# Sixteen per-head stores of the sliding attention's bias table during the difference attention, in place of one store during the projections

## The chip, the cores and the metric

The kernel runs on one core of one Trainium2 chip. Its engines are TensorE (PE, with weight loads as a queue of their own, PEld), VectorE (DVE), ScalarE (ACT), GpSimd (POOL) and SyncE (SP), which here only issues DMA transfers; 16 DMA engines carry them out. The metric is device time in microseconds (us); smaller is better.

## The reference, cut to what matters

Two transformer blocks in fp32 over 2048 tokens of width 1024. The first projects the normed input into eight chunks of 512 columns, runs a difference attention (4 heads) and a dilated attention (8 heads), gates both and adds a projection. The second is a causal sliding-window attention with 16 heads, window 128, a learned bias by distance and a sink for each head. That bias is what the change is about:

```python
def first_block(x, ...):
    u = rms_norm(x, mix_norm_g) @ w_in
    dq, dk, dv, bq, bk, bv, z = jnp.split(u, IN_SPLIT_IDX, axis=-1)
    ...
    a = diff_attention(dq, dk, dv, lam, diff_slopes)     # softmax 0 minus lam * softmax 1, times v
    b = dilated_attention(bq, bk, bv, dil_slopes)
    y = jnp.concatenate([a, b], axis=-1) * jax.nn.silu(z)
    ...
def banded_attention(q, k, v, t5_table, window, sinks):
    ...
    dist = nprev * Q_BLOCK + jnp.arange(Q_BLOCK)[:, None] - jnp.arange(kc)[None, :]
    valid = (dist >= 0) & (dist < window) & (kpos >= 0)
    bias = jnp.take(t5_table, t5_bucket(dist), axis=0)
    s = jnp.where(valid, s + bias, NEG)
    ...
```

The bias depends on the distance alone, so a head's whole bias matrix is made from one vector of 384 numbers: 128 of bias in the middle and −1e30 on both sides.

## The kernel before, in words

The program is a row of phases: `phase_a` (projections), `phase_b1` (difference attention), `phase_b2` (dilated attention), `phase_c` (output projection and gate), `phase_d` (sliding attention) and `phase_e`. Intermediate results go through DRAM tiles named `s_...`. A scheduler with a timeline of its own puts each engine's instructions into a fixed order; semaphores do the rest. All transfers named here are issued by SP, in SP's order, on one queue (`q1` in the profile).

**Projections.** `phase_a` takes the eight chunks in the order dv, bv, dk, dq, bk, bq, z0, z1, and in each chunk 16 tiles of 128 tokens. A tile is 24 matmuls (8 blocks of depth, three products of high and low parts, L190 to L192) into one of four PSUM buffers `psm`. In the second half of a chunk the next chunk's weights are loaded: SP fetches `wraw` (3 buffers, L98), ACT makes the high part (L100) and POOL the low part (L101). In the chunks dv and bv a tile leaves PSUM like this, one store for each part:

```python
            raw = wrp.tile([P, 512], F32, name="wraw")                                       # L97
            nc.sync.dma_start(raw, w_in[0, k * P:(k + 1) * P, ch * 512:(ch + 1) * 512])      # L98
            w = wp.tile([P, 2, 512], F32R, name="w")
            nc.scalar.activation(w[:, 0], raw, AF.Copy)                                      # L100
            ...
            nc.scalar.activation(ev[0], psv, AF.Copy, scale=rs)                              # L110
            nc.vector.scalar_tensor_tensor(ev[1], psv, rs, ev[0].bitcast(F32), ...)          # L111
            for i in range(2):
                nc.sync.dma_start(scr[nm][rows][:, :, i], ev[i].bitcast(F32))                # L113
```

**The bias table.** After the first chunk `phase_a` calls `prep_swa`. It fills `e_vec`, 16 partitions (one for each head) of 384 numbers, and stores it to `s_toep`, 16 x 128 x 384 numbers in DRAM: each head's row is written 128 times, 3 MB in one transfer (L978). `phase_d` reads it skewed by one number from row to row, which turns the repeated vector into the bias matrix.

**Difference attention.** `phase_b1` works through 64 tiles `g` of 128 queries, 16 for each of 4 heads. PE computes scores (L331) from `kst` and `qst`, DVE adds distances and takes the maximum, ACT takes the exponentials, and POOL combines the two softmaxes in halves (L364, L365). Three tiles later PE transposes the result (L375), and pairs of tiles are multiplied by `vt` (L389 to L391). Every fourth tile `finish` loads a gate block `b_sz` (L404), multiplies it on POOL (L406), multiplies the output by it (L418) and stores the output to `s_y` (L419). The next head's `kst` (L305) and `vt` (L311) are loaded at the boundary between heads, `qst` (L318) every fourth tile.

Of the kernel before, what the change touches and what calls it, by code (L numbers as in the profile page):

```python
# [7 lines left out]
F32 = mybir.dt.float32  # L8
# [8 lines left out]
P = 128  # L17
# [251 lines left out]
def phase_b1(tc, c, scr, ndist, sub_g, lam):  # L269
    nc = tc.nc  # L270
    NQ = 4 * NT
    with (
# [27 lines left out]
        def load_k(h, e, j):  # L300
            for i in range(2):
                t = (kp0 if heads["n"] % 22 < 20 else kp1).tile([P, 512], F32R, name="kst")
                heads["n"] += 1
                for half in range(2):
                    nc.sync.dma_start(t[64 * half:64 * half + 64].bitcast(F32),  # L305
                                      scr["dk"][h, e, i][:, j * 512:j * 512 + 512])
                heads[h, "k", e, i, j] = t

        def load_v(h, j):
            t = vp.tile([P, 4, 2, 128], F32R, name="vt")  # L310
            nc.sync.dma_start(t.bitcast(F32),  # L311
                              scr["dv"][j * 512:(j + 1) * 512, h].rearrange("(k p) i w -> p k i w", p=P))
            heads[h, "v", j] = t

        def load_q(h, b):
            for e in range(2):
                t = (qp0, qp1)[b % 2].tile([P, 512], F32R, name="qst")
                nc.sync.dma_start(t.bitcast(F32),  # L318
                                  scr["dq"][h, e].rearrange("s d t -> (s d) t")[:, b * 512:b * 512 + 512])
                qts[h, b, e] = t  # L320

        def scores(g, e, hf):
            h, qt = divmod(g, NT)
            if e == 0 and hf == 0:
                st[g] = {"e": [pool.tile([P, 2, 1024], F32, name="et") for pool in (tp1 if g % 4 == 3 else tp0, tp3 if g % 3 == 2 else tp2)], "l": sp.tile([P, 2], F32, name="l")}
            et = st[g]["e"][e]
            lhs = qts[h, qt // 4, e][:, (qt % 4) * P:(qt % 4 + 1) * P]
            ps = ps_s.tile([P, 1024], F32, name="s_ps")
            for b in range(2):
                for i in range(2):  # L330
                    nc.tensor.matmul(ps[:, b * 512:b * 512 + 512], lhs, heads[h, "k", e, i, 2 * hf + b],  # L331
                                     start=i == 0, stop=i == 1)
            if hf == 0:
                st[g]["mx"] = sp.tile([P, 2], F32, name="mx")
            mx = st[g]["mx"]
            off = 1920 - qt * P + hf * 1024
            nc.vector.tensor_tensor_reduce(  # L337
                et[:, hf], ps, bias[:, off:off + 1024], 1.0,
                -3.0e38 if hf == 0 else mx[:, 0:1], ALU.add, ALU.max, mx[:, hf:hf + 1])

        def exps(g, e):
            slope = DIFF_SLOPES[g // NT]
            et, mx = st[g]["e"][e], st[g]["mx"]
            nm = sp.tile([P, 1], F32, name="nm")
            nc.scalar.activation(nm, mx[:, 1:2], AF.Copy, scale=-slope)
            ev = et.rearrange("p a k -> p (a k)")
            nc.scalar.activation(ev, ev, AF.Exp, bias=nm, scale=slope, accum_out=st[g]["l"][:, e:e + 1])  # L347
# [45 lines left out]
        def evacuate(p):  # L393
            ot = op.tile([P, 256], F32, name="b_ot")
            nc.scalar.activation(ot, outs.pop(p), AF.Copy)
            outs[p, "t"] = ot
# [29 lines left out]
        for g in range(NQ + LT + 5):  # L426
            h, qt = divmod(g, NT)
            if g < NQ and qt == 0:
                for j in range(4):
                    load_v(h, j)  # L430
            if g < NQ and qt % 4 == 1:
                ng = g + 3
                if ng < NQ:
                    load_q(ng // NT, (ng % NT) // 4)
            for s in range(4):
                e, hf = divmod(s, 2)
                if g < NQ:
                    with tc.high_priority(offset=AHEAD) if g < EARLY else nullcontext():
                        scores(g, e, hf)
                    if qt == NT - 1 and h < 3 and hf == 1:  # L440
                        for j in range(4):
                            load_k(h + 1, e, j)
                if 0 <= g - LT < NQ:
                    transposes(g - LT, s)
                p, half = divmod(g - LT - 2, 2)
                if 0 <= p < NQ // 2:
                    for kt in range(8 * half + 2 * s, 8 * half + 2 * s + 2):
                        pv(p, kt)
                if s == FIN and half == 0 and 0 <= p - 1 < NQ // 2:
                    finish(p - 1)  # L450
                if g < NQ and hf == 1:
                    with tc.high_priority(offset=AHEAD) if g < EARLY else nullcontext():
                        exps(g, e)
            if g < NQ:
                with tc.high_priority(offset=AHEAD) if g < EARLY else nullcontext():
                    combine(g)
            p, half = divmod(g - LT - 2, 2)
            if half == 1 and 0 <= p < NQ // 2:
                evacuate(p)
        ssq = c["ssq"].rearrange("p h t -> p (h t)")  # L460
        rsqrt_dve(nc, fp, ssq, 128, ssq)

# [497 lines left out]
def prep_swa(tc, c, scr, table, onehot, sinks, pm):  # L960


    nc = tc.nc
    sk8 = c["const"].tile([P, 16], F32, name="e_sk")
    nc.sync.dma_start(sk8, sinks.broadcast_to([P, 16]))
    nc.vector.tensor_scalar(sk8, sk8, 8.0, None, ALU.mult)
    c["sk8"] = sk8
    with tc.tile_pool(name="p_c", bufs=1) as cp:
        tb = cp.tile([32, 16], F32, name="e_tb")
        nc.sync.dma_start(tb, table)  # L970
        oh = cp.tile([32, P], F32, name="e_oh")
        nc.sync.dma_start(oh, onehot)
        vec = cp.tile([16, 384], F32, name="e_vec")
        nc.vector.memset(vec, -1.0e30)
        ps = pm.tile([P, 512], F32, name="pst")[:16, :P]
        nc.tensor.matmul(ps, tb, oh, start=True, stop=True)
        nc.vector.tensor_scalar(vec[:, 128:256], ps, 8.0, None, ALU.mult)
        nc.sync.dma_start(scr["toep"], vec.unsqueeze(1).broadcast_to([16, P, 384]))  # L978


def phase_d(tc, c, scr, a_w_in):
# [310 lines left out]
def diff_lambda(tc, c, lams):  # L1292
    nc = tc.nc
    c["lam"] = c["const"].tile([P, 1], F32, name="lam")
    with tc.tile_pool(name="l_c", bufs=1) as cp:
        lt = cp.tile([P, 4, 64], F32, name="lt")
        for i, ap in enumerate(lams):
            nc.sync.dma_start(lt[:, i], ap.broadcast_to([P, 64]))
        pr = cp.tile([P, 2, 64], F32, name="lpr")
        for i in range(2):  # L1300
            nc.vector.tensor_mul(pr[:, i], lt[:, 2 * i], lt[:, 2 * i + 1])
        s2 = cp.tile([P, 2], F32, name="ls2")
        nc.vector.reduce_sum(s2, pr, axis=AX.X)
        nc.scalar.activation(s2, s2, AF.Exp)
        nc.vector.tensor_sub(c["lam"], s2[:, 0:1], s2[:, 1:2])
        nc.vector.tensor_scalar(c["lam"], c["lam"], LAM_INIT, None, ALU.add)
# [21 lines left out]
def kernel_body(tc, a, out):  # L1328
    with (
        tc.tile_pool(name="const", bufs=1) as cp,  # L1330
        tc.tile_pool(name="dram", bufs=1, space=DRAM) as dp,
    ):
        c = consts(tc, cp)
        scr = make_scratch(dp)
        phase_a(tc, c, a["x"], a["w_in"], a["mix_norm_g"],
                [a["diff_q_norm_g"], a["diff_k_norm_g"], a["dil_q_norm_g"], a["dil_k_norm_g"]], scr,
                lambda pm: [
                    diff_lambda(tc, c, [a["lambda_q1"], a["lambda_k1"], a["lambda_q2"], a["lambda_k2"]]),
                    prep_swa(tc, c, scr, a["t5_table_2"], a["t_onehot"], a["a_sinks_2"], pm)])
        phase_b1(tc, c, scr, a["t_ndist"], a["diff_sub_norm_g"], c["lam"])  # L1340
        phase_b2(tc, c, scr, a["t_nat"], a["t_res"], a["t_two"])
        phase_c(tc, c, scr, a["x"], a["p"], a["w_out"], a["ple_norm_g"], a["w_ple_gate"], a["w_ple_proj"],
                a["norm_g_2"])
        phase_d(tc, c, scr, a["a_w_in_2"])
        phase_e(tc, c, scr, a["a_w_out_2"], a["final_g_2"], out)
# [29 lines left out]
```

## Time and profile before

| what | value |
|---|---|
| median of 3 runs | 2956.58 us (2953.58 to 2958.02) |
| the profiled execution's own time | 2958.66 us |
| its span | 2956.9 us |
| PE busy | 2878.8 us (97%) |
| DVE, ACT, POOL busy | 1803.7 us (61%), 1562.5 us (53%), 1239.1 us (42%) |
| moved by DMA | 346.00 MB, 117 GB/s in the mean |

The profile is of one execution, which lies 2.1 us above the median. Busy shares are means over all phases. The timelines list one engine's instructions in order of time, with the idle time before an instruction and what ended it in square brackets; the windows give the busy time of each engine in a stretch, and the clock that PE was granted (1.00 is 2.4 GHz, 0.50 is 1.2 GHz).

### The profile page before, as it was taken

The numbers are of one execution on the slowest core, as the hardware profiler recorded it, in microseconds if no ns is written. First come the engines' busy times: TensorE is split into PE (matmuls) and PEld (weight loads), VectorE is DVE, ScalarE is ACT, GpSimd is POOL, SyncE is SP. The second block draws the span as 40 slices with busy tenths as digits, with TensorE's granted clock in tenths as the row PEclk, the third lists the DMA queues.
The fourth block names the chain that finished last, engine by engine and source line by source line (L and its number), as shares of the span: only waits on it lengthen the run. The fifth ranks groups of instructions, "written<-read, shape, count | busy, mean of one in ns | idle before, by whom it ended". The sixth has DMA issues, their size and how long they took to land.

```text
span 2956.9 us, 45164 instructions
## 1 busy us (share of the span) xinstructions
PE 2878.8 (97%) x15554; PEld 2455.2 (83%) x15554; DVE 1803.7 (61%) x4607; ACT 1562.5 (53%) x3480; POOL 1239.1 (42%) x1156
## 2 busy tenths in 40 slices
PE   9999999999999999989999899999999999999998
PEld 7878888888798888878999778888788888888787
DVE  4215556522688888887877654444535756666855
ACT  5222333221588888878989442222345756665621
POOL 1110111001488888864777700000156555555421
PEclk9999999999999999999999899999999999999999
DMA  6663444424314132129786633232554243332552
GB/s 208 116 160 86 122 114 121 96 87 115 121 30 115 46 106 65 51 64 189 143 164 133 180 116 110 77 113 92 183 166 155 86 157 96 109 100 72 156 182 79
DMA packets 410646, 346.00 MB, mean 117 GB/s; under 512 B 89745, under 2 KB 356401, under 8 KB 408497
## 3 DMA queue, kind: packets, MB, share of 16 engines
q1 hardware_dynamic: 388000, 329.24, 40.2%
q10 hardware_dynamic: 20736, 8.65, 1.8%
q0 software_dynamic: 1680, 5.21, 0.7%
q8 instruction: 124, 2.03, 0.3%
q14 instruction: 106, 0.86, 0.1%
HBM read 227.51 MB, written 116.52 MB: 116 GB/s over the span
## 4 chain that ended last, share of the span: by engine, by line
PE 86%; DMA 5%; DVE 3%; ACT 2%; SPq 1%; issue 1%; POOL 0%; DVEq 0%; ACTq 0%; POOLq 0%
PE s_ps L331 8%; PE psm L190 7%; PE psm L192 7%; PE psm L191 7%; PE e_mm L804 5%; PE e_mm L806 5%; PE e_mm L805 5%; PE c_mm L804 4%; PE c_mm L805 4%; PE c_mm L806 4%; PE t_ps L375 3%; PE o_ps L389 2%; PE o_ps L391 2%; PE o_ps L390 2%; PE d_sr L590 2%; PE f_mm L805 2%
## 5 line engine op out<-in xcount | busy, mean ns | idle before, releaser
L190 PE MATMUL psm<-w,hh 128*128 128x512 f32 x1024 | 406.3, 398 | 9.4 <-DVE t L111 8.0
L191 PE MATMUL psm<-w,hl 128*128 128x512 f32 x1024 | 399.5, 391 | 0.0
L192 PE MATMUL psm<-w,hh 128*128 128x512 f32 x1024 | 399.5, 393 | 0.0
L101 POOL TENSOR_TENSOR w<-wraw,w 128x512 fp32r<-128x512 f32 x64 | 81.5, 1294 | 600.2 <-ACT w L100 589.9
L365 POOL TENSOR_TENSOR et<-et 128x1024 f32<-128x1024 f32 x124 | 296.0, 2409 | 0.0
L331 PE MATMUL s_ps<-kst,qst 128*128 128x512 f32 x1024 | 289.7, 407 | 5.5 <-DVE mx L337 3.7
L347 ACT ACTIVATE et<-et,nm 128x2048 f32<-128x2048 f32 x128 | 257.2, 2009 | 5.2
L1026 POOL TENSOR_TENSOR e_wt<-e_raw,e_wt 128x1024 fp32r<-128x1024 f32 x80 | 191.3, 2399 | 111.9 <-ACT e_wt L1025 110.9
L190 PEld LDWEIGHTS psm<-w,hh 128*128 128x128 f32 x1024 | 193.5, 189 | 48.3 <-DVE t L111 8.4
L804 PE MATMUL e_mm<-e_x,e_wt 128*128 128x512 f32 x576 | 228.2, 396 | 1.2 <-DVE e_k L1068 0.8
L806 PE MATMUL e_mm<-e_x,e_wt 128*128 128x512 f32 x576 | 226.8, 394 | 0.0
L192 PEld LDWEIGHTS psm<-w,hh 128*128 128x128 f32 x1024 | 192.9, 189 | 40.9
L805 PE MATMUL e_mm<-e_x,e_wt 128*128 128x512 f32 x576 | 226.6, 393 | 0.0
L191 PEld LDWEIGHTS psm<-w,hl 128*128 128x128 f32 x1024 | 193.7, 189 | 38.2
L331 PEld LDWEIGHTS s_ps<-kst,qst 128*128 128x128 f32 x1024 | 175.9, 190 | 45.3 <-DVE mx L337 18.1
L1127 POOL TENSOR_SCALAR e_es<-e_es,e_l 128x256 f32<-128x256 f32 (+1 forms) x256 | 119.4, 485 | 170.8 <-DVE e_l L1125 118.6
L364 POOL TENSOR_SCALAR et<-et,cc 128x1024 f32<-128x1024 f32 x124 | 138.2, 1129 | 110.3 <-PE psm L192 57.1
L377 DVE TENSOR_TENSOR ptl<-t_ps,pth 128x512 fp32r<-128x512 f32 x256 | 169.4, 684 | 19.9 <-ACT pth L376 16.8
L337 DVE CUSTOM_DVE_ANT_0 et<-s_ps,nd,mx 128x1024 f32<-128x1024 f32 x128 | 163.9, 1280 | 26.5 <-PE s_ps L331 24.7
L1114 DVE CUSTOM_DVE_ANT_0 e_es<-e_s,e_bias,e_sk 128x256 f32<-128x256 f32 (+1 forms) x256 | 117.4, 473 | 102.6 <-PE e_s L1106 71.2
L376 ACT ACTIVATE pth<-t_ps 128x512 fp32r<-128x512 f32 x256 | 143.6, 595 | 44.8 <-PE t_ps L375 41.1
L850 POOL TENSOR_TENSOR c_yn<-c_yn,ssq_sub 128x512 f32<-128x512 f32 x16 | 17.0, 1061 | 354.1 <-DMA c_yn<-s_y 354.1
(268 smaller groups left out, 7848.2 us busy)
## 6 DMA issues: line engine op xcount, KB each, us to landing
e_raw<-in_a_w_in_dram SPq DMA_DIRECT2D x80, 512.0 KB, 3.7
wraw<-in_w_in_dram SPq DMA_DIRECT2D x64, 256.0 KB, 3.5
kst<-s_dk SPq DMA_DIRECT2D x128, 128.0 KB, 4.2
s_xt<-c_at SPq DMA_DIRECT2D x32, 512.0 KB, 6.8
e_x<-s_xt SPq DMA_DIRECT2D x32, 512.0 KB, 7.1
t<-in_x_dram SPq DMA_DIRECT2D x32, 256.0 KB, 5.4
s_dv<-t SPq DMA_DIRECT2D x32, 256.0 KB, 3.3
s_bv<-t SPq DMA_DIRECT2D x32, 256.0 KB, 3.6
```

What stands on the lines that cost most here:

```text
L190: nc.tensor.matmul(ps, ah, cur[k][:, 0], start=k == 0, stop=False)
L191: nc.tensor.matmul(ps, al, cur[k][:, 0], start=False, stop=False)
L192: nc.tensor.matmul(ps, ah, cur[k][:, 1], start=False, stop=k == KD - 1)
L331: nc.tensor.matmul(ps[:, b * 512:b * 512 + 512], lhs, heads[h, "k", e, i, 2 * hf + b], start=i == 0, stop=i == 1)
L337: nc.vector.tensor_tensor_reduce(et[:, hf], ps, bias[:, off:off + 1024], 1.0, -3.0e38 if hf == 0 else mx[:, 0:1], ALU.add, ALU.max, mx[:, ...
L347: nc.scalar.activation(ev, ev, AF.Exp, bias=nm, scale=slope, accum_out=st[g]["l"][:, e:e + 1])
L365: nc.gpsimd.tensor_sub(es[0][:, hf], es[0][:, hf], es[1][:, hf])
L377: nc.vector.tensor_sub(tl[:, :, qi], pt, th[:, :, qi].bitcast(F32))
L804: nc.tensor.matmul(ps, ah, bh, start=first, stop=False)
L805: nc.tensor.matmul(ps, al, bh, start=False, stop=False)
L806: nc.tensor.matmul(ps, ah, bl, start=False, stop=last)
L1026: nc.gpsimd.tensor_sub(w[:, 1], raw, w[:, 0].bitcast(F32))
```

## The change

`e_vec` moves to a pool of its own, `early`, that lives through the projections and the difference attention. The store of `prep_swa` is taken out, and 16 stores take its place in the loop of `phase_b1`: at the end of every even tile from 8 to 38, one head's row, written 128 times (192 KB) from one partition. `keep_in_program_order` keeps each where it is written relative to SP's neighbours.

```diff
@@ phase_b1, end of the loop over g
             p, half = divmod(g - LT - 2, 2)
             if half == 1 and 0 <= p < NQ // 2:
                 evacuate(p)
+            if g % 2 == 0 and 8 <= g < 40:
+                hd = (g - 8) // 2
+                tc.keep_in_program_order(nc.sync.dma_start(
+                    scr["toep"][hd], c["vec"][hd:hd + 1].unsqueeze(1).broadcast_to([1, P, 384])))
@@ prep_swa
-        vec = cp.tile([16, 384], F32, name="e_vec")
+        vec = c["early"].tile([16, 384], F32, name="e_vec")
         nc.vector.memset(vec, -1.0e30)
...
         nc.vector.tensor_scalar(vec[:, 128:256], ps, 8.0, None, ALU.mult)
-        nc.sync.dma_start(scr["toep"], vec.unsqueeze(1).broadcast_to([16, P, 384]))
+    c["vec"] = vec
@@ kernel_body
-        phase_a(tc, c, ...)
-        phase_b1(tc, c, scr, a["t_ndist"], a["diff_sub_norm_g"], c["lam"])
+        with tc.tile_pool(name="early", bufs=1) as c["early"]:
+            phase_a(tc, c, ...)
+            phase_b1(tc, c, scr, a["t_ndist"], a["diff_sub_norm_g"], c["lam"])
```

SP's order between the first and the second chunk of the projections, before (`s_dv` are stores of the first chunk, `s_bv` of the second, `wraw` the weights to come):

```order
L113 DMA s_dv<-t_1169 512x1x128
L98 DMA wraw<-in_w_in_dram 128x512 x3
L978 DMA s_toep<-e_vec 2048x1x384
L113 DMA s_dv<-t_1204 512x1x128
L98 DMA wraw<-in_w_in_dram 128x512
L113 DMA s_dv<-t_1205 512x1x128
L98 DMA wraw<-in_w_in_dram 128x512 x2
L113 DMA s_bv<-t_1270 1024x1x64
```

and after:

```order
L113 DMA s_dv<-t_1172 512x1x128
L98 DMA wraw<-in_w_in_dram 128x512 x3
L113 DMA s_dv<-t_1207 512x1x128
L98 DMA wraw<-in_w_in_dram 128x512
L113 DMA s_dv<-t_1208 512x1x128
L98 DMA wraw<-in_w_in_dram 128x512 x4
L113 DMA s_bv<-t_1272 1024x1x64
```

The store has left the queue, and two weight loads more stand ahead of the first store of the second chunk.

SP's order in the difference attention, from the first two `b_sz` loads to the `kst` loads of the second head, before:

```order
L404 DMA b_sz<-s_sz 128x4x128 x2
L318 DMA qst<-s_dq 128x512 x4
L419 DMA s_y_138<-b_an 128x4x128
L404 DMA b_sz<-s_sz 128x4x128
L318 DMA qst<-s_dq 128x512 x2
L419 DMA s_y_138<-b_an 128x4x128
L404 DMA b_sz<-s_sz 128x4x128
L305 DMA kst<-s_dk 64x512 x20
```

and after:

```order
L404 DMA b_sz<-s_sz 128x4x128
L462 DMA s_toep<-e_vec 128x1x384
L404 DMA b_sz<-s_sz 128x4x128
L462 DMA s_toep<-e_vec 128x1x384
L318 DMA qst<-s_dq 128x512 x4
L419 DMA s_y_138<-b_an 128x4x128
L462 DMA s_toep<-e_vec 128x1x384
L404 DMA b_sz<-s_sz 128x4x128
L318 DMA qst<-s_dq 128x512 x2
L419 DMA s_y_138<-b_an 128x4x128
L462 DMA s_toep<-e_vec 128x1x384
L404 DMA b_sz<-s_sz 128x4x128
L462 DMA s_toep<-e_vec 128x1x384
L305 DMA kst<-s_dk 64x512 x20
```

A store of one head now stands ahead of each of these `b_sz` loads but the first; the six loads that follow here have one ahead of them too, and the boundary to the third head has its two stores in the same places.

POOL's order around the sixth `b_sz` load, before:

```order
L418 TENSOR_TENSOR b_an<-b_an,b_sz 128x512
L364 TENSOR_SCALAR et<-et,cc 128x1024 x2
L406 TENSOR_TENSOR b_sz<-b_sz,g_6576 128x512
L365 TENSOR_TENSOR et<-et 128x1024 x2
L364 TENSOR_SCALAR et<-et,cc 128x1024 x2
```

and after:

```order
L418 TENSOR_TENSOR b_an<-b_an,b_sz 128x512
L364 TENSOR_SCALAR et<-et,cc 128x1024 x2
L365 TENSOR_TENSOR et<-et 128x1024
L406 TENSOR_TENSOR b_sz<-b_sz,g_6578 128x512
L365 TENSOR_TENSOR et<-et 128x1024
L364 TENSOR_SCALAR et<-et,cc 128x1024 x2
```

The multiply by the gate block has moved behind the first half of L365; the same holds for the seventh and the eighth load, and the other places keep their order. PE's order is the same in both kernels.

## Rows read from the trace of the kernel before

**Rows 1.** The page: busy time by engine, and shares of the chain.
```profile
PE 2878.8 (97%) x15554; PEld 2455.2 (83%) x15554; DVE 1803.7 (61%) x4607; ACT 1562.5 (53%) x3480; POOL 1239.1 (42%) x1156
...
PE 86%; DMA 5%; DVE 3%; ACT 2%; SPq 1%; issue 1%; POOL 0%; DVEq 0%; ACTq 0%; POOLq 0%
```

**Rows 2.** DMA issues, 110 to 160: operation, count, size, us from issue to landing.
```profile
s_toep<-e_vec SPq DMA_DIRECT2D x1, 3072.0 KB, 35.5
```

**Rows 3.** Timeline of SP at the store: start us, us, engine, line, operation, count.
```profile
114.01 0.65 SPq L978 DMA_DIRECT2D s_toep<-e_vec  x1
```

**Rows 4.** Timeline of ACT, idle time and its releaser in brackets.
```profile
150.98 0.63 ACT L100 ACTIVATE w<-wraw 128x512 fp32r<-128x512 f32 x1 [25.48 <-DMA wraw<-in_w_in_dram]
```

**Rows 5.** Timeline of PE behind its stop in the second chunk.
```profile
154.56 0.80 PE L190 MATMUL psm<-w,hh 128*128 128x512 f32 x1 [8.03 <-DVE t L111]
```

**Rows 6.** Windows: stretch, us, busy PE, PEld, DVE, ACT, POOL; PEclk; DMA; GB/s.
```profile
154.50:160.30 5.80, 5.74 (x14) 4.48 (x15) 1.98 (x4) 0.95 (x2) 0.00 (x0) 0.50 1.04 258
160.30:200.00 39.70, 39.70 (x177) 32.84 (x175) 5.26 (x7) 4.83 (x7) 0.00 (x0) 1.00 0.52 132
...
1323.20:1328.00 4.80, 0.01 (x1) 0.00 (x0) 1.04 (x2) 1.06 (x4) 1.26 (x1) 0.96 1.01 244
1328.00:1331.00 3.00, 2.95 (x12) 2.78 (x13) 0.33 (x1) 0.60 (x1) 0.00 (x0) 0.50 1.01 230
...
880.00:1100.00 220.00, 217.75 (x1433) 190.39 (x1432) 187.91 (x350) 179.35 (x336) 189.01 (x113) 1.00 0.32 89
```

**Rows 7.** DMA queue, 120 to 145: packets, MB, share of 16 engines.
```profile
q1 hardware_dynamic: 1591, 2.44, 91.4%
```

**Rows 8.** DMA queue, 630 to 640, where only `s_sz` stores run.
```profile
q1 hardware_dynamic: 288, 0.52, 13.6%
```

**Rows 9.** Timeline of SP in the difference attention.
```profile
781.26 0.93 SPq L404 DMA_DIRECT2D b_sz<-s_sz  x2
...
914.53 0.51 SPq L404 DMA_DIRECT2D b_sz<-s_sz  x1
...
1026.56 13.65 SPq L305 DMA_DIRECT2D kst<-s_dk  x20
...
1092.66 0.50 SPq L404 DMA_DIRECT2D b_sz<-s_sz  x1
```

**Rows 10.** Tile `b_sz`: ten loads from 775 to 1110, then the one of 914.53.
```profile
DMA to landing us min/median/max: 2.9/3.4/4.7
...
DMA to landing us min/median/max: 4.7/4.7/4.7
```

**Rows 11.** Timeline of POOL in the difference attention.
```profile
788.40 1.30 POOL L406 TENSOR_TENSOR b_sz<-b_sz,g 128x512 f32<-128x512 f32 x1
789.65 4.75 POOL L365 TENSOR_TENSOR et<-et 128x1024 f32<-128x1024 f32 x2
...
883.39 1.29 POOL L406 TENSOR_TENSOR b_sz<-b_sz,g 128x512 f32<-128x512 f32 x1 [1.24 <-DMA b_sz<-s_sz]
...
920.99 1.30 POOL L406 TENSOR_TENSOR b_sz<-b_sz,g 128x512 f32<-128x512 f32 x1
...
924.43 4.80 POOL L365 TENSOR_TENSOR et<-et 128x1024 f32<-128x1024 f32 x2
...
1097.13 1.30 POOL L406 TENSOR_TENSOR b_sz<-b_sz,g 128x512 f32<-128x512 f32 x1
1098.38 4.77 POOL L365 TENSOR_TENSOR et<-et 128x1024 f32<-128x1024 f32 x2
```

**Rows 12.** Timeline of PE: transposes (L375) and a score (L331).
```profile
792.49 1.03 PE L375 MATMUL t_ps<-id,et 128*128 128x128 f32 x8
...
929.96 0.60 PE L375 MATMUL t_ps<-id,et 128*128 128x128 f32 x4
...
1038.66 0.47 PE L331 MATMUL s_ps<-kst,qst 128*128 128x512 f32 x1 [0.63 <-DMA kst<-s_dk]
...
1103.42 0.60 PE L375 MATMUL t_ps<-id,et 128*128 128x128 f32 x4
```

More of the change, by code (lines that the diff above doesn't have):

```diff
@@ L1334, in kernel_body @@
         scr = make_scratch(dp)
[L1335 to L1339, printed above, removed]
-        phase_b1(tc, c, scr, a["t_ndist"], a["diff_sub_norm_g"], c["lam"])
+        with tc.tile_pool(name="early", bufs=1) as c["early"]:
+            phase_a(tc, c, a["x"], a["w_in"], a["mix_norm_g"],
+                    [a["diff_q_norm_g"], a["diff_k_norm_g"], a["dil_q_norm_g"], a["dil_k_norm_g"]], scr,
+                    lambda pm: [
+                        diff_lambda(tc, c, [a["lambda_q1"], a["lambda_k1"], a["lambda_q2"], a["lambda_k2"]]),
+                        prep_swa(tc, c, scr, a["t5_table_2"], a["t_onehot"], a["a_sinks_2"], pm)])
+            phase_b1(tc, c, scr, a["t_ndist"], a["diff_sub_norm_g"], c["lam"])
         phase_b2(tc, c, scr, a["t_nat"], a["t_res"], a["t_two"])
```

## The prediction

> **What bounds the kernel now.** I read the page first: TensorE is busy 97% of the span and makes up 86% of the chain that ended last [rows 1]. So a change gains only where PE stands still or runs slowly, and loses wherever PE is made to wait. Next I looked for the store that the change moves, in the DMA issues of its stretch: one issue of 3072 KB that takes 35.5 us to land [rows 2], sent at 114.0 [rows 3]. What it does to others is read from the timelines, going from the transfer to the engine that waits for it. ACT sits idle for 25.48 us until a block of raw weights lands, and converts it at 150.98 [rows 4]; the evacuations of the second chunk stand behind that conversion in ACT's order. Four PSUM buffers fill and PE stops for 8.03 us before 154.56 [rows 5]. The windows show the sequel: from 154.5 to 160.3 the granted clock is 0.50 and 14 matmuls fill 5.8 us, where the stretch behind it has 177 in 39.7 us at 1.00 [rows 6], 0.224 us each, so the 14 are worth 3.1 us and 2.7 us are lost. **The store costs 8.0 + 2.7 = 10.7 us of PE time today.** PE is full from there to the end of the projections, so all of it counts.
>
> **What is removed.** With the store gone from this place, SP's queue holds only weight loads and `s_dv` stores there, and the raw weights no longer wait behind 3 MB. ACT's two conversions move ahead of the next evacuation in its order; 1.3 us of work, hidden since all of it is now early. I credit the whole −10.7 us; the bounds are 0 (something else holds the second chunk) and −10.7.
>
> **What a piece costs.** This decides the case. Before has no store of one partition, so the price has to be bounded. While the big store runs alone (120 to 145), its 1591 packets keep the 16 engines busy 91.4% [rows 7]: 0.914 x 25 us x 16 / 1591 = 230 ns for 1536 B, 6.7 GB/s for each engine and 98 GB/s together. A store from 128 partitions takes 13.6% of 16 engines in 10 us for 0.52 MB [rows 8]: 24 GB/s for each engine. So the engines are full and yet 3.6 times too slow: something behind them is shared. The source of the big store lies on 16 partitions alone, and 98 GB/s is what four unhindered engines move (4 x 24). I read it as four outlets, one for each four partitions, of 24.4 GB/s each, or 26.7 without the idle 8.6%. A piece reads 196,608 B from one partition: through one outlet, 196,608 / 26.7e3 = 7.4 us. The Trainium skill, page "SBUF — State Buffer", section "Door 1: The DMA port swizzle (why `[64,N]` ≈ `[32,N]`)", says that partitions 0 to 3 share one of 16 ports; at its 27.2 GB/s a port, an estimate is 7.2 us a piece, and the trace's 98 GB/s from 16 partitions agrees with four such ports. The low end is 2.0 us, the piece at the big store's 98 GB/s, which holds if the limit is not in the source. The high end is 8.2 us, at the 24 GB/s of one engine. **I take 7.4 us**, because it follows from the only row in which this data is read. The big store was 16 pieces at once over four outlets (35.5 us to land), the new ones are 16 x 7.4 = 118 us in all; only their place can make that cheap.
>
> **What waits behind a piece.** All 16 engines take part in each piece and serve one queue in order, so what SP issues next lands 7.4 us later. That a load behind the store suffers in this way is seen in [rows 4]. The order of the changed kernel puts a piece directly ahead of a `b_sz` load in nine places, a tile of queries of `vt` once between them. POOL's multiply by that load (L406) stands in POOL's order ahead of the L364/L365 combine, and PE's transposes (L375) need the combine. POOL already waits for such a landing once, at 883.39 [rows 11]. So each place has a cover: from landing to the multiply, and from the end of the L365 pair to the transposes. Loads land 3.4 us after issue in the median of ten, the one of 914.53 after 4.7 [rows 10].
> First: the second load of 781.26 [rows 9] goes out at 781.7 and lands at 785.1; the multiply runs at 788.40, 3.3 us later; the first of the L365 pair from 789.65 ends at 792.0 [rows 11] and the transposes start at 792.49 [rows 12]: 0.5. Cover 3.8, stall 7.4 − 3.8 = 3.6 us.
> Fourth: landed at 919.2 [rows 9, 10], multiply at 920.99, pair done at 929.23 [rows 11], second transposes at 929.96 [rows 12]: cover 1.8 + 0.7 = 2.5, stall 4.9, and 1.4 more for the `vt` load that also goes ahead (512 KB at 16 x 24 GB/s): 6.3.
> Ninth: landed at 1096.1, multiply at 1097.13, pair's first half done at 1100.8, transposes at 1103.42, in the same groups: cover 3.7, stall 3.7.
> The others by the same reading: second 0.5, third 4.7, eighth 4.4. In the fifth to seventh the multiply is moved behind one L365 and delays only the other; this adds 2.4 us of cover, and stalls of 3.7, 2.3 and 2.0 remain. **Sum of nine: 31.2 us.**
>
> **The head boundaries.** Two pieces stand ahead of the `kst` loads of heads 1 and 2. Before, 20 issues of 13.65 us begin at 1026.56 [rows 9], 0.68 each, and PE waits 0.63 us for one at 1038.66 [rows 12], so there is no cover. Two pieces from 1022.3 end at 1037.1; the loads start 10.5 us late, catch up 0.34 us each (0.68 of issue, 128 KB in 0.34), and are 6.4 late at the twelfth; PE is by then 2.0 late through the seventh stall: **4.4 us more**. At the first boundary the same sum leaves 4.8 against the third stall's 4.7: 0.1 us.
>
> **The clock.** After a stop of 4.8 us at 1323.2 the next 3.0 us are granted 0.50 [rows 6], which loses 1.5 us. Seven of the stalls are 3.6 us or longer: 7 x 1.5 = **10.5 us**; the bounds are 0 and 2.7 for each.
>
> **At no cost**: the other five pieces that stand ahead of `qst` and `vt` loads (these are sent a head or a block of queries ahead of their use); the issue time on SP (0.65 us each, SP waits for others anyway); the earlier memset (DVE has nothing to do then); the readers of the table, which start in the sliding attention, two phases later. PE's own idle time in this stretch is 2.25 us of 220 [rows 6]; I give back 2 of it, since a late PE finds its data ready.
>
> **Sum**: −10.7 + 31.2 + 4.4 + 0.1 + 10.5 − 2 = +33.5 us. On the profiled 2958.66 that is 2992.2; this execution lies 2.1 over the median, so 2990 in the measure of the median. With T = 6.0 for a piece (nine stalls 11.5 less, boundary 1.4 less, three clock drops fewer) it would be 2972, with 8.2 it would be 3000; half the covers mis-read gives ± 5. Its own range is 2967 to 3007.
>
> **Rivals.**
> A, faster: the limit is not in the source row but in the 16 engines' writing, so a piece takes 2.0 us. Only the fourth place is short of cover then (2.0 + 1.4 − 2.5 = 0.9): −10.7 + 0.9 = −9.8, 2947 (2944 to 2950). For it speaks that `b_sz` has 3 to 7 us of cover nearly everywhere; against it, that a source on 128 partitions runs 3.6 times faster through the same engines [rows 7, 8]. 0.14. The Trainium skill, page "DMA: Bandwidth & Descriptors", section "Anatomy of one DMA — SWDGE (gpsimd) path", has a fit of 2.0 us plus bytes / 436 GB/s, by which a piece would be 2.45 us, an estimate; by that rule the time would come out in this case, but for the big store it gives 9.2 us where the trace has 35.5.
> B, no change: a piece costs about 4.4 us, or POOL's gaps take up more than I read. Stalls of 1.1, 0.0, 1.7, 3.3, 0.7, 0, 0, 1.4 and 0.7 and a clock drop or two then eat the gain: 2957 (2951 to 2963). 4.4 us is the point from which the sign turns. 0.08.
> C, slower by more: the stop in the second chunk stays because the weights wait for a buffer and not for the store; the gain is nil and the time about 3001. This is inside the likeliest case's range and its chance with it.
> That the change does not do what it says is out: the order has all 16 pieces in the difference attention.
>
> **How the numbers follow.** Likeliest with C, slower, 0.78, at 2990. Same 0.08, faster 0.14. 0.2% of this time is 6 us, about what a measurement can tell from no change. The range from 2955 to 3010 leaves out A, a bit of B and the top of the likeliest: 0.20.
>
> **What would show it.** Right: after 146 no stop of PE and clock 1.00; each `s_toep` store lands 8 to 10 us after issue; POOL idle at L406 `<-DMA b_sz` for several us in most of the nine places, where one wait of 1.24 us stands now; PE waits for L365 in 780 to 1110 at seven to nine places, with 0.50 behind them. Wrong: pieces landing within 4 us, or landing late with POOL not waiting, because `b_sz` goes round them.

## The result and the profile after

The changed kernel takes 2979.78 us in the median of 4 runs (2977.30 to 2982.14), beside 2956.97 us for the kernel before on the same chip; the ratio is 1.0072 with a 95% interval of 1.0060 to 1.0084. **It is slower by 23 us.** The forecast was 2990 with a range of 2955 to 3010: the sign and the mechanism held, and the loss was forecast at 33.5 us, half as much again as it is. One term of the sum, the stalls of PE behind the pieces, carries nearly all of that. The profiled execution took 2980.42 us, its span 21.7 us more than the span before.

The gain came as forecast. The windows of the stretch in which PE had stood still and run at 0.50 [rows 6] now read (us, then busy PE, PEld, DVE, ACT, POOL, granted clock, DMA share, GB/s):

```profile
147.00:154.50 7.50, 7.50 (x34) 6.19 (x33) 1.50 (x2) 1.15 (x2) 0.00 (x0) 1.00 0.32 81
154.50:160.30 5.80, 5.80 (x27) 4.82 (x26) 0.75 (x1) 0.69 (x1) 0.00 (x0) 1.00 0.42 106
```

PE is full at 1.00, 27 matmuls in the stretch that held 14. On ACT's timeline the two conversions that waited 25.48 us for their weights [rows 4] come 30 us earlier:

```profile
120.43 0.63 ACT L100 ACTIVATE w<-wraw 128x512 fp32r<-128x512 f32 x1 [3.39 <-DMA wraw<-in_w_in_dram]
121.79 0.63 ACT L100 ACTIVATE w<-wraw 128x512 fp32r<-128x512 f32 x1 [0.73 <-DMA wraw<-in_w_in_dram]
```

The loss is in the difference attention. PE's order is the same in both kernels, so the same 2507 matmuls can be set side by side: they fill 739.2 to 1170.4 in the changed kernel (first fence: the window, then PE's waits as total us, times, longest) and 750 to 1150 in the kernel before (second fence):

```profile
739.20:1170.40 431.20, 402.04 (x2507) 347.71 (x2506) 338.49 (x624) 315.77 (x577) 327.91 (x195) 0.96 0.39 76
...
PE t_ps L375 <- POOL et L365: 19.6, 8, 3.4
PE s_ps L331 <- DMA kst<-s_dk: 5.0, 6, 2.0
PE s_ps L331 <- DVE mx L337: 2.6, 6, 0.7
PE t_ps L375 <- DVE ptl L377: 1.9, 1, 1.9
```

```profile
750.00:1150.00 400.00, 392.16 (x2507) 340.39 (x2506) 337.63 (x624) 313.94 (x577) 328.02 (x195) 1.00 0.26 74
...
PE s_ps L331 <- DVE mx L337: 3.7, 8, 1.1
PE t_ps L375 <- DVE ptl L377: 2.2, 1, 2.2
PE s_ps L331 <- DMA kst<-s_dk: 1.6, 3, 0.6
PE o_ps L389 <- ACT pth L376: 0.2, 1, 0.2
```

They take 31.2 us longer: 9.9 us more of busy PE and 21.3 us more of waits. A wait that was not there at all, of the transposes for POOL's combine, is now the largest. The timelines show how it comes about. On POOL, in four of the nine places:

```profile
781.29 1.28 POOL L406 TENSOR_TENSOR b_sz<-b_sz,g 128x512 f32<-128x512 f32 x1 [3.77 <-DMA b_sz<-s_sz]
...
884.11 1.29 POOL L406 TENSOR_TENSOR b_sz<-b_sz,g 128x512 f32<-128x512 f32 x1 [7.95 <-DMA b_sz<-s_sz]
...
923.34 1.30 POOL L406 TENSOR_TENSOR b_sz<-b_sz,g 128x512 f32<-128x512 f32 x1 [4.80 <-DMA b_sz<-s_sz]
...
1120.72 1.30 POOL L406 TENSOR_TENSOR b_sz<-b_sz,g 128x512 f32<-128x512 f32 x1 [4.61 <-DMA b_sz<-s_sz]
```

and on PE, a few us behind each:

```profile
784.92 1.59 PE L375 MATMUL t_ps<-id,et 128*128 128x128 f32 x8 [3.24 <-POOL et L365]
...
889.97 1.09 PE L375 MATMUL t_ps<-id,et 128*128 128x128 f32 x8 [3.25 <-POOL et L365]
...
929.22 1.97 PE L375 MATMUL t_ps<-id,et 128*128 128x128 f32 x8 [3.42 <-POOL et L365]
...
1124.39 0.66 PE L375 MATMUL t_ps<-id,et 128*128 128x128 f32 x4 [1.90 <-POOL et L365]
```

These answer [rows 11, 12]: the places are the same, and the two outer ones can be read across the kernels. The transposes of 792.49 now start at 784.92, 7.6 us earlier; those of 1103.42 start at 1124.39, 21.0 us later. So 28.5 us are lost between the first stall's end and the ninth's, after 10.7 were gained and the first stall had taken some back.

Behind the stalls of 3.0 to 3.4 us, and at the second head boundary (1050), the clock is granted at its lower level for a few us. Behind those of 1.0 to 2.6 us it stays at 1.00; the row of 1005.57 follows the longest of them:

```profile
784.90:788.30 3.40, 3.38 (x13) 3.00 (x14) 0.00 (x0) 2.31 (x4) 3.40 (x3) 0.57 0.60 163
...
929.20:932.50 3.30, 3.28 (x13) 2.95 (x14) 0.00 (x0) 1.20 (x2) 3.30 (x2) 0.55 0.92 104
...
1005.57:1009.00 3.43, 3.43 (x22) 3.03 (x23) 2.33 (x5) 2.65 (x4) 3.43 (x3) 1.00 0.00 0
...
1050.00:1054.00 4.00, 3.32 (x12) 2.69 (x13) 1.58 (x4) 0.87 (x3) 0.00 (x0) 0.50 0.71 226
```

The price of a piece is in the DMA queue between 845 and 850, while a piece runs alone (packets, MB, share of 16 engines), with the engines' busy tenths in 40 slices:

```profile
DMA  7799773099973709997770799973379993730999
...
q1 hardware_dynamic: 91, 0.14, 88.8%
```

91 packets of 1536 B in 5 us are 28 GB/s from engines that are busy 88.8% of the time. In the trace the 128 packets of this piece run from 843.9 to 851.1: **7.2 us**, where 7.4 was forecast. Between 775 and 1120 the DMA issues say what that does (KB each, median us from issue to landing):

```profile
s_toep<-e_vec SPq DMA_DIRECT2D x15, 192.0 KB, 9.0
s_y<-b_an SPq DMA_DIRECT2D x8, 256.0 KB, 2.3
b_sz<-s_sz SPq DMA_DIRECT2D x8, 256.0 KB, 9.2
```

A `b_sz` load lands 9.2 us after its issue, where it took 3.4 [rows 10]. On SP's timeline this piece and the load behind it are

```profile
842.56 0.51 SPq L462 DMA_DIRECT2D s_toep<-e_vec  x1
843.11 0.59 SPq L404 DMA_DIRECT2D b_sz<-s_sz  x1
```

and the packets of that load move from 850.6 to 851.9.

### The profile page after: what moved, and what is told of

It is laid out like the page before. It is cut to its first block, busy times and chain, and to the rows that moved or that the text cites. A ratio compares the mean times of both kernels' runs of the same rounds, so it can differ in the third digit from the quotient of the medians.

```text
span 2978.6 us, 45176 instructions
## 1 busy us (share of the span) xinstructions
PE 2888.9 (97%) x15554; PEld 2464.4 (83%) x15554; DVE 1806.3 (61%) x4607; ACT 1565.4 (53%) x3480; POOL 1241.4 (42%) x1156
## 5 line engine op out<-in xcount | busy, mean ns | idle before, releaser
L331 PE MATMUL s_ps<-kst,qst 128*128 128x512 f32 x1024 | 294.8, 413 | 7.6 <-DMA kst<-s_dk 5.0
L365 POOL TENSOR_TENSOR et<-et 128x1024 f32<-128x1024 f32 x124 | 296.2, 2413 | 0.0
L331 PEld LDWEIGHTS s_ps<-kst,qst 128*128 128x128 f32 x1024 | 180.4, 194 | 47.4 <-DVE mx L337 14.8
L337 DVE CUSTOM_DVE_ANT_0 et<-s_ps,nd 128x1024 f32<-128x1024 f32 x128 | 156.0, 1219 | 34.3 <-PE s_ps L331 23.5
```

Of the source, the lines that this page charges most:

```text
L337: nc.vector.tensor_tensor_reduce(et[:, hf], ps, bias[:, off:off + 1024], 1.0, -3.0e38 if hf == 0 else mx[:, 0:1], ALU.add, ALU.max, mx[:, ...
L365: nc.gpsimd.tensor_sub(es[0][:, hf], es[0][:, hf], es[1][:, hf])
```

## The experiments

**Without the stores** (`e1_no_store`). All 16 are left out, and with them the bias table: the sliding attention reads its biases from another DRAM tile.

```diff
-            if g % 2 == 0 and 8 <= g < 40:
-                hd = (g - 8) // 2
-                tc.keep_in_program_order(nc.sync.dma_start(scr["toep"][hd], ...))
-        toep = scr["toep"].rearrange("h r u -> h (r u)")[...]
+        toep = scr["dk"].rearrange("a b c d s -> (a b c d s)")[0:16 * P * 384].rearrange("(h w) -> h w", h=16)[...]
```

> The changed kernel without any of the 16 stores; the sliding attention reads another DRAM tile of the same shape, so its biases are wrong and its transfers the same. My theory: nothing but the stores moved time, so this is the kernel before less the stop in the second chunk of the projections: 10.7 us faster than before, about 2946, and 33 us faster than the changed kernel. Rival: the gain in the projections is given back later by waits that were there anyway; then it is within 3 us of before, 2954 to 2957.

Measured: 2948.22 us beside 2958.65 for before, ratio 0.9962 (0.9949 to 0.9975), 10.4 us faster. PE's waits between 775 and 1120 are

```profile
PE s_ps L331 <- DVE mx L337: 1.0, 3, 0.5
PE o_ps L389 <- ACT pth L376: 0.2, 1, 0.2
```

The stop in the projections was worth what was read, and it isn't given back. The stores alone make the loss, which against this kernel is some 33 us.

**The source on four partitions, 4 apart** (`e2_four_outlets`). The vector is held 8 times over 128 partitions (that edit is left out here) and each store reads four of them, 32 rows from each. Places, sizes and, in this stretch, the orders of PE, ACT and POOL are those of the changed kernel.

```diff
+                lo = 64 * (hd // 8) + 32 * (hd // 4 % 2) + hd % 4
...
-                    scr["toep"][hd], c["vec"][hd:hd + 1].unsqueeze(1).broadcast_to([1, P, 384])))
+                    scr["toep"][hd].rearrange("(k r) u -> k r u", k=4),
+                    c["vec"][lo:lo + 13:4].unsqueeze(1).broadcast_to([4, 32, 384])))
```

> The changed kernel, same 16 stores at the same places and of the same size, but each reads its row from four partitions that lie 4 apart (the vector is held 8 times over 128 partitions) instead of one. My theory (four adjacent partitions share one outlet of about 27 GB/s, and the stalls follow from a piece's 7 us): a piece takes about 2 us, the loads behind it land about 1.5 us later than without, the covers hold nearly everywhere: 2946 to 2950, 10 faster than before. Rival: it is the place and the number of the transfers, their fixed cost, that makes the loads late: then little changes and it stays at 2970 to 2980.

Measured: 2947.99 us beside 2958.65, ratio 0.9964 (0.9951 to 0.9976), 10.7 us faster. The packets of a piece run from 840.5 to 843.1, 2.6 us, and of PE's waits in the stretch one kind is left:

```profile
PE s_ps L331 <- DVE mx L337: 3.3, 6, 1.1
```

Sixteen stores at the very same places cost nothing once each is short. Neither their number nor their place is the cause by itself.

**The source on four adjacent partitions** (`e3_one_outlet`). The same kernel, but the four partitions stand in a row (one `b_sz` load goes ahead of a `vt` load instead of behind it; nothing else differs in the orders).

```diff
-                lo = 64 * (hd // 8) + 32 * (hd // 4 % 2) + hd % 4
+                lo = 64 * (hd // 8) + 4 * (hd % 8)
...
-                    c["vec"][lo:lo + 13:4].unsqueeze(1).broadcast_to([4, 32, 384])))
+                    c["vec"][lo:lo + 4].unsqueeze(1).broadcast_to([4, 32, 384])))
```

> As e2_four_outlets, the same shapes of transfers, but the four partitions that a store reads are adjacent, 4c to 4c+3. My theory: they share one outlet, so a piece still takes about 7 us and the time is that of the changed kernel, 2975 to 2983. Rival: what is slow is reading one partition's row again and again; with four partitions it is as fast as e2_four_outlets, 2946 to 2950.

Measured: 2988.67 us beside 2958.65, ratio 1.0101 (1.0086 to 1.0116), 30 us slower, and so 41 us over its twin. Between 845 and 850, while a piece runs (busy tenths of the 16 engines, and GB/s, in 40 slices):

```profile
DMA  3132222222222222222222222222225468971457
GB/s 37 12 37 25 25 25 25 25 25 25 25 25 25 25 25 25 25 25 25 25 25 25 25 25 25 25 25 25 25 41 139 102 176 250 274 201 29 86 193 217
```

Four engines work and move 25 GB/s together, what one moves unhindered [rows 8]. The piece runs from 843.0 to 851.0, 8.0 us. Two transfers of the same shape, with some four packets under way at a time in each, differ by three times through the partition numbers alone. So four adjacent partitions do share one outlet, and it isn't the reading of one row over and over that is slow. The range of 2975 to 2983 was missed by 5.7 us; 1.7 of them are this chip, whose kernel before is slower by that much too. A piece is 0.8 us longer than in the changed kernel, and PE's waits for L365 and `kst` add up to 28.2 us in place of 24.6.

**Pieces of 7 us, sent behind the gate-block loads** (`e4_behind`). The 16 stores of the changed kernel, in pairs, each pair right behind a `b_sz` load; `PLACES` numbers these loads from 0.

```diff
+PLACES = [0, 1, 2, 5, 6, 9, 10, 11]
...
+                if p // 2 in PLACES:
+                    for hd in range(2 * PLACES.index(p // 2), 2 * PLACES.index(p // 2) + 2):
+                        tc.keep_in_program_order(nc.sync.dma_start(
+                            scr["toep"][hd], c["vec"][hd:hd + 1].unsqueeze(1).broadcast_to([1, P, 384])))
                 nc.gpsimd.tensor_mul(szt, szt, g08.unsqueeze(1).broadcast_to([P, 4, 128]))
...
-            if g % 2 == 0 and 8 <= g < 40:
-                ...
```

> The changed kernel with its 16 stores from one partition unchanged in size and source, but sent in pairs right behind a gate-block load (calls 0, 1, 2, 5, 6, 9, 10, 11 of it), where only loads of queries follow for the next 30 us. My theory: the pieces cost nothing in themselves, what costs is what is queued behind them; still 7 us each, but 2946 to 2950, with POOL not waiting for the gate block. Only the second gate block has two pieces ahead of it, which may cost up to 10 us: then 2955. Rival: 118 us of busy engines slow every other load and the time stays above 2965.

Measured: 2960.94 us beside 2958.65, ratio 1.0004 (0.9994 to 1.0014), no change. The one place that was named as a risk took the whole gain: the first pair stands between the first two `b_sz` loads. SP, POOL and PE there:

```profile
772.24 0.38 SPq L405 DMA_DIRECT2D b_sz<-s_sz  x1
772.66 1.20 SPq L409 DMA_DIRECT2D s_toep<-e_vec  x2
773.90 4.48 SPq L405 DMA_DIRECT2D b_sz<-s_sz  x1
...
790.76 1.26 POOL L411 TENSOR_TENSOR b_sz<-b_sz,g 128x512 f32<-128x512 f32 x1 [11.33 <-DMA b_sz<-s_sz]
...
794.38 1.97 PE L376 MATMUL t_ps<-id,et 128*128 128x128 f32 x8 [10.80 <-POOL et L366]
```

The estimate for it, up to 10 us, was short: PE stands for 10.8 us, and with the clock behind it that would be the 13 us by which this run is slower than the kernel without stores. The next run puts that to the test.

**The same, with that pair sent later** (`e5_behind_late`).

```diff
-PLACES = [0, 1, 2, 5, 6, 9, 10, 11]
+PLACES = [1, 2, 5, 6, 9, 10, 11, 13]
```

> As e4_behind, but the pair that stood between the first two gate-block loads (call 0) is sent later (call 13); all other pairs stay. My theory: the 13 us that e4_behind lost against the kernel without stores were one stall of 10.8 us of PE and the slower clock behind it, made by this pair alone, so the time comes down to that of the kernel without stores, 10 us faster than before, with 16 pieces of 7 us still in the difference attention. Rival: busy DMA engines slow the other loads in general; then it stays within 4 us of before.

Measured: 2949.61 us beside 2961.36, ratio 0.9957 (0.9942 to 0.9971), 11.8 us faster. POOL's waits for the gate block between 760 and 1130 are down to

```profile
POOL b_sz L411 <- DMA b_sz<-s_sz: 1.6, 2, 1.4
```

Here 16 pieces, in eight pairs of some 14 us each, run for 112 us of the difference attention, and PE waits 0.7 us for POOL's combine. What costs is what is queued behind a piece and needed soon.

**The store in one piece at its old place, the source on 128 partitions** (`e6_wide_source`). The kernel before with the vector held 8 times.

```diff
-        vec = cp.tile([16, 384], F32, name="e_vec")
+        tbx = cp.tile([32, 16, 8], F32, name="e_tbx")
+        nc.vector.tensor_copy(tbx, tb.unsqueeze(2).broadcast_to([32, 16, 8]))
+        vec = cp.tile([P, 384], F32, name="e_vec")
...
-        nc.tensor.matmul(ps, tb, oh, start=True, stop=True)
+        nc.tensor.matmul(ps, tbx.rearrange("p h k -> p (h k)"), oh, start=True, stop=True)
...
-        nc.sync.dma_start(scr["toep"], vec.unsqueeze(1).broadcast_to([16, P, 384]))
+        nc.sync.dma_start(scr["toep"].rearrange("h (k r) u -> (h k) r u", k=8),
+                          vec.unsqueeze(1).broadcast_to([P, 16, 384]))
```

> The kernel before, the store in one piece at its old place in the projections, with one thing changed: the vector is held on 128 partitions (8 in a row for each head, each written 16 times) instead of 16. My theory: the 35.5 us were the four outlets of 16 partitions; over all outlets 3 MB take 8 to 10 us at the 24 GB/s of each engine, the weights behind it land in time, PE does not stop: 10 us faster than before. Rival: the many writes to DRAM hold the store to 98 GB/s, and nothing changes. Between them: the store is faster but the weights still come late, 3 to 7 us faster.

Measured: 2947.30 us beside 2961.36, ratio 0.9957 (0.9941 to 0.9974), some 13 us faster. The DMA issue that answers [rows 2], and ACT's conversion that answers [rows 4]:

```profile
s_toep<-e_vec SPq DMA_DIRECT2D x1, 3072.0 KB, 10.5
...
132.00 0.63 ACT L100 ACTIVATE w<-wraw 128x512 fp32r<-128x512 f32 x1 [1.21 <-DMA wraw<-in_w_in_dram]
```

The same 3 MB to the same DRAM rows land in 10.5 us in place of 35.5, and PE has no wait between 100 and 200. The writes to DRAM do not hold the store to 98 GB/s. **This version and `e5_behind_late` both beat both kernels**; their intervals don't tell them apart, and this one needs neither a longer-lived pool nor a place in another phase.

**Two partitions, 4 apart** (`e8_two_outlets`). A piece between the short and the long one, at the places of the changed kernel; the edit is shown against the run with four partitions 4 apart.

```diff
-                    scr["toep"][hd].rearrange("(k r) u -> k r u", k=4),
-                    c["vec"][lo:lo + 13:4].unsqueeze(1).broadcast_to([4, 32, 384])))
+                    scr["toep"][hd].rearrange("(k r) u -> k r u", k=2),
+                    c["vec"][lo:lo + 5:4].unsqueeze(1).broadcast_to([2, 64, 384])))
```

> As e2_four_outlets, 16 stores at the places of the changed kernel, but each reads from two partitions 4 apart. Two engines at 24 GB/s make 192 KB in 4.1 us, between the 2.6 us of e2_four_outlets and the 7.2 us of the changed kernel. My theory after the first runs (a load behind a piece of 7.2 us came 5.8 later, so one behind 4.1 us comes some 2.8 later, and the covers are as read): stalls at the fourth load and at the second head boundary only, 3 to 5 us with the clock: 5 to 8 us faster than before. Rival, as in the prediction: the whole duration counts, 4.4 us is where gain and loss meet: within 2 us of before.

Measured: 2956.08 us beside 2961.36, ratio 0.9985 (0.9974 to 0.9995), 4.4 us faster by the ratio. A piece takes 4.4 us (840.4 to 844.8). PE's waits between 760 and 1130:

```profile
PE t_ps L375 <- POOL et L365: 4.6, 6, 2.0
...
PE s_ps L331 <- DMA kst<-s_dk: 2.7, 2, 2.5
```

The interval reaches from 1.5 to 7.7 us, so it touches both figures, 5 to 8 and within 2. At the 4.4 us that the prediction named as the turning point there is still a gain, so the turn lies higher; but six places stall a little, not the fourth alone.

## Why the prediction was right in sign and too large

**The gain**, −10.7 us: right. The windows above show it, and the kernel without stores gives 10.4.

**The price of a piece**, 7.4 us, read from a store on 16 partitions: right, 7.2. The reading behind it, one outlet for four adjacent partitions at 24 to 27 GB/s, was only argued there; the twin runs show it. The Trainium skill, page "SBUF — State Buffer", section "Door 1: The DMA port swizzle (why `[64,N]` ≈ `[32,N]`)", says just this of adjacent partitions, and its 27.2 GB/s a port agrees with 196,608 B in 7.2 us, 27.3 GB/s. Rival A falls with it: this store isn't held by the engines' writing. The fit beside rival A, from the Trainium skill, page "DMA: Bandwidth & Descriptors", section "Anatomy of one DMA — SWDGE (gpsimd) path", is stated for transfers that GpSimd issues, and these are SP's; by it a piece is estimated at 2.45 us to landing and 3 MB at 9.2. The trace differs for a source on one partition (9.0 us), and for 128 partitions it comes near (10.5 us for the 3 MB).

**The stalls behind a piece**, 31.2 us in nine places: the places and the path (load, POOL's multiply, combine, transposes) were right, and the size was not. The term was mis-sized at the step "what SP issues next lands 7.4 us later". It landed 9.2 − 3.4 = 5.8 us later. Where the piece runs from 843.9, the parts can be read: the piece takes 7.2 us and not 7.4; the load is issued 0.55 us behind it; and its first packets move at 850.6, when the first engines are through with the piece, half a us before the last. That is 1.3 of the 1.6 us. With 5.8 in place of 7.4 the forecast's own covers give 2.0 + 0 + 3.1 + 4.7 + 2.1 + 0.7 + 0.4 + 2.8 + 2.1 = 17.9 us, and measured are **19.6 us**. Place by place, in order, PE waited 3.2, 0, 3.3, 3.4, 1.0, 2.6, 1.1, 3.0 and 1.9, where 3.6, 0.5, 4.7, 6.3, 3.7, 2.3, 2.0, 4.4 and 3.7 were forecast. So the smaller delay explains the sum, and the single places less well: the sixth waits 2.6 and not 0.7 (its load landed after 10.7 us), and the fourth, with the `vt` load ahead, 3.4 and not 4.7.

**The head boundaries**, 4.5 us: PE's waits for `kst` grew from 1.6 to 5.0, 3.4 us; all 5.0 stand at the second boundary, as forecast.

**The clock**, 10.5 us: the same matmuls keep PE busy 402.0 us in place of 392.2, 9.9 us more. That the size is met is luck in part. The forecast had seven drops of 1.5 us behind stalls of 3.6 us or longer (its nine places have six such stalls; the 4.4 us at the second head boundary would be the seventh). No stall was that long, and four, of 3.0 to 3.4 us, drew the lower clock. Matched one by one, the matmuls behind these four lose 1.0 to 1.6 us each, 4.8 together. The waits for `kst` at the second boundary, for which the forecast has one drop at most, lose 3.6, and 1.2 lie ahead of the first stall.

**Given back**, 2 us: over the same matmuls PE's waits for DVE and ACT fell from 6.1 us (3.7, 2.2 and 0.2) to 4.5, which is 1.6: right. **The sum** in spans: −10.7 + 19.6 + 3.4 + 9.9 − 1.6 = +20.6; the spans differ by 21.7, and the 1.1 us between are not placed. Beside the forecast, the stalls are 11.6 us less, and the other terms together 1.3.

Two figures of the forecast do not follow from its own covers: in rival B the first stall is 0.6 us and not 1.1, and with pieces of 6.0 us the nine stalls are 11.7 less and not 11.5. Neither changes which way it points or moves it by a us.

Rival B, the turn at 4.4 us: the run with two partitions shows it to lie higher, between 4.4 us (4.4 faster) and 7.2 us (23 slower). Rival C, a stop that stays, is out by the windows. The forecast of how the profile would look held: landings of 9 us, POOL waiting for `b_sz`, PE for L365 in eight of nine places. The lower clock stood behind four of them, not all.

## What to carry to other kernels

Before a long store is cut up and moved, ask why it is long: here a vector on 16 partitions went out at 98 GB/s, and holding it on all 128 made the store three times faster where it stood and gave the whole gain. Short transfers from one partition are as slow as that partition's outlet, and a queue served in order passes the delay to the next load; send them behind the loads that are needed soon, not ahead. And price a stall of the tensor engine twice, by its length and by the slower clock behind it: here the stalls of 3.0 to 3.4 us cost 1.0 to 1.6 us more that way, those up to 2.6 us nothing.

## What was not expected of the hardware

A store that occupies only 4 of the 16 engines delays a load behind it as much as one that occupies all: in the run with four adjacent partitions the engines are busy two tenths, yet the kernel lost more than the changed one (30 us and 23). The trace shows it for the load behind the piece of 843.0: 384 of its 512 packets are through at 845.0, while the piece still runs, and the last 128, the same quarter of all as the piece's engines are, move only from 850.6 to 851.7. And a stop of PE of 3.2 us was followed by a granted clock of 0.57 over 3.4 us, nearly as much as the stop of 4.8 us was (0.50 over 3.0 us [rows 6]); behind the stop of 8.0 us it was 0.50 over 5.8 us.
